# Order of the work around five RMS norms in a two-layer fp32 encoder: weight tiles ahead of the norm, modulation units behind it

## The chip, the cores and the metric

The kernel runs on one core of one Trainium2 chip. Its time is device microseconds from start to end of one execution, and runs are compared by their median.

## The reference

Two layers, 256 tokens, width 2048, everything in fp32. Each layer makes six vectors of 2048 values from a conditioning vector c, normalizes, modulates, mixes with two kinds of attention, and applies an MLP with a squared ReLU:

```python
c_act = jax.nn.silu(c)
for layer in range(DEPTH):                       # DEPTH = 2
    mod = c_act @ ada_w[layer] + ada_b[layer]    # 2048 -> 6 * 2048
    sh1, sc1, g1, sh2, sc2, g2 = split(mod, 6)
    h = rmsnorm(x, norm_mix[layer]) * (1 + sc1) + sh1
    proj = h @ w_in[layer]                       # 2048 -> 4608
    ...                                          # differential and windowed attention
    x = x + g1 * (concatenate([out_a, out_b]) @ w_out[layer])        # 2048 -> 2048
    h2 = rmsnorm(x, norm_mlp[layer]) * (1 + sc2) + sh2
    x = x + g2 * (square(relu(h2 @ w_up[layer])) @ w_down[layer])    # 2048 -> 8192 -> 2048
return rmsnorm(x, final_norm)
```

rmsnorm(x, g) is x / sqrt(mean(x^2) + 1e-6) * g over the width.

## The kernel before

x lies in SBUF with the features on partitions: 16 chunks of 128 features x 256 tokens, held as 8 pairs of chunks. A weight comes in raw tiles of 128 x 1024 fp32 (0.52 MB), issued on the queue of SyncE (SP) into a ring of six buffers. To keep fp32 accuracy each raw tile is split in two: ScalarE (ACT) casts it to `whi` (L367) and VectorE (DVE) makes the rest `wlo` = raw - whi (L368). Four such split tiles fit at a time. h is split alike into hi and lo. For each chunk and 128 columns, TensorE (PE) runs one matmul of `whi` against hi and lo side by side (512 columns, L408) and one of `wlo` against hi (256 columns, L410). A tile carries 512 output columns of two chunks, so 16 matmuls; a block of 512 columns over eight chunks is four tiles, 64 matmuls, and its four sums leave PSUM by ACT (L487) and DVE (L488).

The six modulation vectors of the two layers are computed beside this on DVE, in 384 units. One unit loads a 128 x 1024 tile of `ada_w` into the same ring of six buffers and reduces it against c_act with one long DVE instruction and a read of its accumulator (both L255). A layer's vectors are needed stage by stage, so units are mixed into the gemms: `pace(goal, tiles)` works out how many units go with each weight tile so that `goal` units are done when the stage ends, and `feed` issues them. The goals are the table GOALS, for the in-projection's two parts, w_out and the four parts of the MLP of each layer. Of a layer's 192 units the first 96 serve its mixer and the other 96 its MLP.

A stage ends in `residual` (L761: x = acc * gate + x on DVE), and the following norm squares x on ACT (L530), adds six of the eight squared pairs on DVE (L534), sums over features on PE with a matmul against a matrix of 1/2048 (L541), and takes (mean+eps)^-0.5 with Ln and Exp on ACT (L550, L551) and one Newton step of four DVE operations (L552 to L555). Then `modulated` makes h of pair i: x times r (L585, L587), hi and the unrounded v on ACT (L589, L593; v on DVE, L591, in layer 1), and lo = v - hi on DVE (L595, L599). There are five norms: at the start, before the MLP and before the mixer of layer 1, before that layer's MLP, and at the end. The names used below for the stages are: w_out0, w_up0 (the MLP of layer 0 up to its first goal of 160 units), mixer 1, w_out1, w_up1.

A list scheduler gives the order of the instructions on each engine from the order in which they were written and from priorities (the norm and h are written under a high priority); on the engine they run in that order, and a semaphore wait holds all that stands behind it.

Of the kernel before, what the change touches and what calls it, by code (L numbers as in the profile page):

```python
# [16 lines left out]
ALU = mybir.AluOpType  # L17
# [25 lines left out]
RAWB, WB = 6, 8  # L43


GOALS = [((72, 96, 120), (160, 204, 248, 304)), ((316, 326, 352), (384, 384, 384, 384))]
# [76 lines left out]
def encoder_trunk(  # L123
# [258 lines left out]

    def gemm(w, c0, width, rows, acts, kind, rate, banks=None, begin=True, end=True):
# [7 lines left out]
        tiles, index = w  # L391
# [57 lines left out]
        for u in range(0, n, per):  # L449
            raw = rawp.tile([P, RAW], F32, tag="raw", name=nm("raw"))  # L450
            nc.sync.dma_start(raw, tiles[index[(c0, rows[u])]])
            if acts[u][1]:
                hl = split(raw, RAW)
            for j in range(per):
                cs = slice(j * width, (j + 1) * width)
                if acts[u + j][1]:
                    held.append((u + j, hl[0][:, cs], hl[1][:, cs]))
                else:
                    held.append((u + j, raw[:, cs], None))
# [64 lines left out]
    ssq = [None, None]  # L524

    def square_sum(i):

        n = NCH // 2
        sq = tmp() if i else bslot(F32)[:, 0]
        nc.scalar.activation(sq, X[i], AF.Square)  # L530
        if i == 0:
            ssq[1] = sq
        elif i < SQ_ADDED:
            nc.vector.tensor_add(ssq[1], ssq[1], sq)  # L534
        if i < SQ_ADDED - 1:
            return
        if i == SQ_ADDED - 1:
            ssq[0] = misc_bank()
            sq = ssq[1]
        for j in range(2):  # L540
            nc.tensor.matmul(  # L541
                ssq[0][:, 0, :], lhsT=mean_d, rhs=sq[:, j, :],
                start=i == SQ_ADDED - 1 and j == 0, stop=i == n - 1 and j == 1, skip_group_check=True)

    def norm_x():

        ms = ssq[0][:, 0, :]
        t = bslot(F32)
        r, y, a = t[:, 0, 0, :], t[:, 0, 1, :], t[:, 1, 0, :]
        nc.scalar.activation(a, ms, AF.Ln, bias=eps)  # L550
        nc.scalar.activation(y, a, AF.Exp, scale=-0.5)  # L551
        nc.vector.tensor_mul(a, y, y)  # L552
        nc.vector.scalar_tensor_tensor(a, ms, EPS, a, op0=ALU.add, op1=ALU.mult)
        nc.vector.tensor_scalar(a, a, -0.5, 1.5, op0=ALU.mult, op1=ALU.add)
        nc.vector.tensor_mul(r, y, a)  # L555
        return r
# [16 lines left out]
    def modulated(l, sec, i, rstd, cols):  # L573
        whole = (l, sec, i) in WHOLE
        t = tmp()
        if whole:
            v = v0 = single()
        else:
            hl = bslot()
            v = tmp()  # L580
        hi, lo = (None, None) if whole else (hl[:, 0], hl[:, 1])
        for j in range(2):
            G, sh = cols[j]
            if i == 0:
# [3 lines left out]
            if not whole:  # L588
                nc.scalar.activation(hi[:, j, :], t[:, j, :], AF.Identity, scale=G, bias=sh)  # L589
            if (l, sec) in V_DVE:  # L590
                nc.vector.tensor_scalar(v[:, j, :], t[:, j, :], G, sh, op0=ALU.mult, op1=ALU.add)  # L591
            else:
                nc.scalar.activation(v[:, j, :], t[:, j, :], AF.Identity, scale=G, bias=sh)  # L593
            if i == 0 and not whole:
                nc.vector.tensor_tensor(lo[:, j, :], v[:, j, :], hi[:, j, :].bitcast(F32), op=ALU.subtract)  # L595
# [114 lines left out]
    def grouped_gemm(w, blocks, groups, get_act, goal, capped=None):  # L710
# [3 lines left out]
        for gi, gn in enumerate(groups):  # L714
# [7 lines left out]
            acts = [get_act(kk) for kk in rows]  # L722
            k0 += gn
            for bi, (c0, width, kind, finish) in enumerate(blocks):
# [7 lines left out]
                banks = gemm(w, c0, width, rows, acts, kind, r)  # L732
                if last:
# [32 lines left out]
    def mixer(l, groups, goals):  # L766
        with tc.high_priority():
            if l == 0:
                for i in range(NCH // 2):
                    square_sum(i)  # L770
            rstd = norm_x()
# [53 lines left out]
        grouped_gemm(w_in[l], blocks, groups, get_h, goals[0], (l, 0))  # L825
# [3 lines left out]
        rate = pace(goals[2], 32)  # L829
        for part in range(2):  # L830
# [3 lines left out]
            for c0 in range(0, D, w):  # L834
                banks = gemm(w_out[l], c0, w, rows, acts, kind, rate)
                residual(banks, l, 2, c0 // (2 * P), part == 1, kind)

    def mlp(l, groups, goals):
# [94 lines left out]
```

## Time and profile before

| | us |
|---|---|
| median of three runs | 2317.24 |
| the three runs | 2321.05, 2309.28, 2317.24 |
| the profiled execution, whole | 2310.85 |
| its span in the trace | 2309.1 |
| PE busy in the span | 2191.3 (95%) |
| DVE busy | 1808.1 (78%) |
| ACT busy | 1061.2 (46%) |

Busy is the time in which an engine ran at least one instruction. PE is close to full over the whole, but DVE is not evenly used: the units fill it in the first two thirds of the program, and after unit 384 it has less to do. A value of idle time ahead of an instruction says what ended that idle time.

### The profile page before, as it was taken

Reading aid. Unit: us, or ns where it says so; the run is one execution under the profiler, and the core shown is the slowest. Engines: PE = TensorE matmul, PEld = TensorE weight load, DVE = VectorE, ACT = ScalarE, POOL = GpSimd, SP = SyncE. Lnnn points to the kernel's source line nnn. Section 1 sums busy time; section 2 is a strip of 40 time slices with the busy share of each in tenths; the row PEclk is TensorE's granted clock in tenths of the full one; section 3 lists DMA queues with packets and bytes.
Section 4 is the critical chain, followed back from the end, with each engine's and each line's share of the span. In section 5 each row is a group of like instructions: output and inputs, shape, how many; then the busy total and the mean of one; then the engine's idle time right before and its main releaser. Section 6 shows DMA issues by size and latency. Waiting matters only on the chain.

```text
span 2309.1 us, 33300 instructions
## 1 busy us (share of the span) xinstructions
PE 2191.3 (95%) x12540; PEld 1894.8 (82%) x12540; DVE 1808.1 (78%) x2698; ACT 1061.2 (46%) x1521; POOL 0.2 (0%) x4
## 2 busy tenths in 40 slices
PE   5879999789999999999989999997999999999997
PEld 4768888678888888888878977886888888888886
DVE  6899899998888788988888578999886555565454
ACT  2436565355443334444336467534444334454442
POOL 0000000000000000000000000000000000000000
PEclk8989999999999999999999999999999999999999
DMA  8887675898678999999885754686886565555653
GB/s 324 327 311 275 217 255 201 293 329 301 204 274 316 316 317 328 314 338 348 312 302 192 246 182 157 211 290 236 297 282 233 185 195 186 192 191 187 195 184 110
DMA packets 162450, 585.96 MB, mean 254 GB/s; under 512 B 18289, under 2 KB 18801, under 8 KB 162289
## 3 DMA queue, kind: packets, MB, share of 16 engines
q1 hardware_dynamic: 162288, 583.83, 73.0%
q8 instruction: 99, 1.62, 0.3%
q14 instruction: 63, 0.51, 0.1%
HBM read 581.66 MB, written 2.10 MB: 253 GB/s over the span
## 4 chain that ended last, share of the span: by engine, by line
PE 83%; DVE 4%; ACT 2%; issue 1%; DMA 1%; ACTq 0%; DVEq 0%
PE acc L408 48%; PE acc L410 25%; PE acc L381 2%; PE acc L379 2%; PE acc L380 2%; PE misc L616 1%; DVE wlo L368 1%; PE lg L631 1%; DVE araw L255 1%; DVE x L761 1%; PE misc L608 1%; PE lg L680 1%; DMA raw<-in_w_up_dram 0%; ACT whi L367 0%; PE misc L562 0%
## 5 line engine op out<-in xcount | busy, mean ns | idle before, releaser
L408 PE MATMUL acc<-b,whi 128*128 128x512 f32 x4992 | 1742.5, 395 | 38.8 <-DVE b L595 29.4
L410 PE MATMUL acc<-b,wlo 128*128 128x256 f32 x4992 | 1377.1, 281 | 5.0 <-DVE wlo L368 4.8
L408 PEld LDWEIGHTS acc<-b,whi 128*128 128x128 f32 x4992 | 933.4, 188 | 249.2 <-issue 38.0
L367 ACT CAST whi<-raw 128x1024 fp32r<-128x1024 f32 x711 | 726.7, 1052 | 871.8 <-PE acc L408 540.0
L368 DVE TENSOR_TENSOR wlo<-raw,whi 128x1024 fp32r<-128x1024 f32 x711 | 851.9, 1222 | 321.5 <-ACT whi L367 319.4
L410 PEld LDWEIGHTS acc<-b,wlo 128*128 128x128 f32 x4992 | 943.5, 189 | 25.1 <-DVE wlo L368 11.9
L255 DVE CUSTOM_DVE_ANT_0 araw<-araw,c_act,vecs 128x1024 f32<-128x1024 f32 x192 | 249.1, 1303 | 43.5 <-DMA araw<-in_ada_dram 43.3
L255 DVE CUSTOM_DVE_ANT_0 araw<-araw,c_act,mod 128x1024 f32<-128x1024 f32 x192 | 249.1, 1303 | 35.5 <-DMA araw<-in_ada_dram 35.1
L761 DVE SCALAR_TENSOR_TENSOR x<-acc,mod,x 128x256 f32<-128x256 f32 x256 | 112.9, 480 | 24.1 <-PE acc L410 22.1
L379 PE MATMUL acc<-b,whi 128*128 128x256 f32 x320 | 92.1, 291 | 2.9 <-ACT whi L367 2.9
L380 PE MATMUL acc<-b,whi 128*128 128x256 f32 x320 | 91.8, 290 | 0.0
L381 PE MATMUL acc<-b,wlo 128*128 128x256 f32 x320 | 89.4, 293 | 2.5 <-DVE wlo L368 2.4
L487 ACT COPY tmp<-acc 128x256 f32<-128x256 f32 x120 | 44.5, 372 | 64.6 <-PE acc L410 64.3
L488 DVE TENSOR_TENSOR tmp<-tmp,acc 128x256 f32<-128x256 f32 x152 | 62.0, 418 | 14.0 <-ACT tmp L487 13.8
L498 ACT CAST b<-tmp 128x512 fp32r<-128x512 f32 x72 | 44.8, 623 | 49.8 <-DVE tmp L854 48.9
L379 PEld LDWEIGHTS acc<-b,whi 128*128 128x128 f32 x320 | 62.6, 196 | 4.9 <-ACT whi L367 3.3
L381 PEld LDWEIGHTS acc<-b,wlo 128*128 128x128 f32 x320 | 61.1, 197 | 5.3 <-DVE wlo L368 4.0
L380 PEld LDWEIGHTS acc<-b,whi 128*128 128x128 f32 x320 | 62.7, 196 | 1.1 <-issue 1.0
L380 PE MATMUL acc<-wlo,b 128*128 128x512 f32 (+1 forms) x152 | 56.6, 372 | 3.1 <-DVE wlo L368 3.0
L530 ACT ACTIVATE tmp<-x 128x512 f32<-128x512 f32 x35 | 21.7, 631 | 75.7 <-DVE x L761 68.3
L381 PE MATMUL acc<-whi,b 128*128 128x512 f32 (+1 forms) x152 | 55.9, 367 | 0.0
L499 DVE TENSOR_TENSOR b<-tmp,b 128x512 fp32r<-128x512 f32 x72 | 49.3, 688 | 7.1 <-ACT b L498 6.2
(156 smaller groups left out, 1258.6 us busy)
## 6 DMA issues: line engine op xcount, KB each, us to landing
araw<-in_ada_dram SPq DMA_DIRECT2D x384, 512.0 KB, 5.2
raw<-in_w_up_dram SPq DMA_DIRECT2D x256, 512.0 KB, 4.5
raw<-in_w_down_dram SPq DMA_DIRECT2D x256, 512.0 KB, 4.6
raw<-in_w_in_dram SPq DMA_DIRECT2D x144, 512.0 KB, 4.7
raw<-in_w_out_dram SPq DMA_DIRECT2D x64, 512.0 KB, 4.7
x<-in_x_dram SPq DMA_DIRECT2D x8, 256.0 KB, 5.0
out_dram<-tmp SPq DMA_DIRECT2D x8, 256.0 KB, 2.3
b<-in_diff_lambda_dram SPq DMA_DIRECT2D x1, 256.0 KB, 7.8
```

What stands on the lines that cost most here:

```text
L255: nc.vector.tensor_tensor_reduce(raw, raw, c_act[:, hf * RAW : (hf + 1) * RAW], scale=scale, scalar=m[:, ch : ch + 1] if hf else vecs[:, b ...
L367: nc.scalar.copy(hi, raw)
L368: nc.vector.tensor_tensor(lo, raw, hi.bitcast(F32), op=ALU.subtract)
L379: nc.tensor.matmul(o, lhsT=lhi, rhs=rhi, start=first, stop=False, skip_group_check=True)
L380: nc.tensor.matmul(o, lhsT=lhi, rhs=rlo, start=False, stop=False, skip_group_check=True)
L381: nc.tensor.matmul(o, lhsT=llo, rhs=rhi, start=False, stop=last, skip_group_check=True)
L408: nc.tensor.matmul(bank, lhsT=hi[:, fs], rhs=act[:, :, aj, :], start=first, stop=False, skip_group_check=True)
L410: nc.tensor.matmul(bank[:, 1, :], lhsT=lo[:, fs], rhs=act[:, 0, aj, :], start=False, stop=last, skip_group_check=True)
L488: nc.vector.tensor_add(tj, tj, b[:, 1, :])
L498: nc.scalar.copy(hl[:, 0], src)
L499: nc.vector.tensor_tensor(hl[:, 1], src, hl[:, 0].bitcast(F32), op=ALU.subtract)
L761: nc.vector.scalar_tensor_tensor(x[:, j, :], sums, g[j], x[:, j, :], op0=ALU.mult, op1=ALU.add)
```

## The change

- `load_ahead` issues and splits the first two raw tiles of w_up or of the next layer's w_in behind the last gemm block of w_out or w_down, ahead of that block's residual.
- No units go with that last block; the goals move, and the pace of the blocks before it is worked out over fewer tiles (28 of 32, 48 of 64).
- In the first block behind a norm (four tiles in w_up0), all that is written after h of pair 0 is queued behind the last ACT and the last DVE operation of the norm and of that h (`issue_after`).
- h of a pair is made when a tile needs it, two chunks ahead (`OnDemand`, LOOK), in place of a whole group at once.
- The Newton step takes three DVE operations, hi and v of pair 0 are made on DVE, the squares of the last pair are taken in two halves, and the first norm adds nothing on DVE: PE sums all 16 chunks.

```diff
-GOALS = [((72, 96, 120), (160, 204, 248, 304)), ((316, 326, 352), (384, 384, 384, 384))]
+AHEAD = 2
+LOOK = 2
+GOALS = [((72, 96, 116), (160, 208, 252, 296)), ((312, 324, 352), (384, 384, 384, 384))]
...
+    def load(w, c0, row, whole=False):
+        tiles, index = w
+        raw = rawp.tile([P, RAW], F32, tag="raw", name=nm("raw"))
+        nc.sync.dma_start(raw, tiles[index[(c0, row)]])
+        return (raw, None) if whole else split(raw, RAW)
+    class OnDemand:
+        def __init__(self, get, rows):
+            self.get, self.rows = get, rows
+        def __getitem__(self, i):
+            return self.get(self.rows[i])
+    def load_ahead(w, c0):
+        for row in range(0, 2 * AHEAD, 2):
+            ahead[(id(w), c0, row)] = load(w, c0, row)
...
         for u in range(0, n, per):
-            raw = rawp.tile([P, RAW], F32, tag="raw", name=nm("raw"))
-            nc.sync.dma_start(raw, tiles[index[(c0, rows[u])]])
-            if acts[u][1]:
-                hl = split(raw, RAW)
+            acts[min(u + LOOK, n - 1)]
+            key = (id(w), c0, rows[u])
+            hl = ahead.pop(key) if key in ahead else load(w, c0, rows[u], not acts[u][1])
...
+    @contextmanager
+    def behind(ops):
+        with ExitStack() as stack:
+            for op in ops:
+                stack.enter_context(tc.issue_after(op.ins))
+            yield
+    def square_sum(i, added=SQ_ADDED):
         n = NCH // 2
+        sq = tmp() if i or not added else bslot(F32)[:, 0]
+        if i == n - 1:
+            for j in range(2):
+                nc.scalar.activation(sq[:, j, :], X[i][:, j, :], AF.Square)
...
         nc.scalar.activation(a, ms, AF.Ln, bias=eps)
-        nc.scalar.activation(y, a, AF.Exp, scale=-0.5)
-        nc.vector.tensor_mul(a, y, y)
-        nc.vector.scalar_tensor_tensor(a, ms, EPS, a, op0=ALU.add, op1=ALU.mult)
-        nc.vector.tensor_scalar(a, a, -0.5, 1.5, op0=ALU.mult, op1=ALU.add)
-        nc.vector.tensor_mul(r, y, a)
+        last_op[1] = nc.scalar.activation(y, a, AF.Exp, scale=-0.5)
+        nc.vector.scalar_tensor_tensor(a, ms, EPS, y, op0=ALU.add, op1=ALU.mult)
+        nc.vector.scalar_tensor_tensor(a, a, -0.5, y, op0=ALU.mult, op1=ALU.mult)
+        last_op[0] = nc.vector.scalar_tensor_tensor(r, a, 1.5, y, op0=ALU.add, op1=ALU.mult)
         return r
...
+            if not whole and i == 0:
+                nc.vector.tensor_scalar(hi[:, j, :], t[:, j, :], G, sh, op0=ALU.mult, op1=ALU.add)
+            elif not whole:
                 nc.scalar.activation(hi[:, j, :], t[:, j, :], AF.Identity, scale=G, bias=sh)
-            if (l, sec) in V_DVE:
-                nc.vector.tensor_scalar(v[:, j, :], t[:, j, :], G, sh, op0=ALU.mult, op1=ALU.add)
+            if (l, sec) in V_DVE or i == 0:
+                last_op[0] = nc.vector.tensor_scalar(v[:, j, :], t[:, j, :], G, sh, op0=ALU.mult, op1=ALU.add)
...
+            acts = OnDemand(get_act, rows)
+            if gi == 0 and norm is not None:
+                acts[0]
+                front.enter_context(behind(last_op))
...
                 banks = gemm(w, c0, width, rows, acts, kind, r)
+                front.close()
...
-        rate = pace(goals[2], 32)
+        rate = pace(goals[2], 28)
...
-                banks = gemm(w_out[l], c0, w, rows, acts, kind, rate)
+                final = part == 1 and c0 + w == D
+                banks = gemm(w_out[l], c0, w, rows, acts, kind, 0.0 if final else rate)
+                if final:
+                    load_ahead(w_up[l], 0)
...
-            rate = pace(goal, n * 2)
+            rate = pace(goal, n * 2 - (n // 2 if final else 0))
...
+                quiet = final and nb == 3
+                banks = gemm(w_down[l], nb * 512, 512, rows, acts, "s", 0.0 if quiet else rate)
+                if quiet and l + 1 < DEPTH:
+                    load_ahead(w_in[l + 1], KA)
```

The instructions on DVE at the norm before w_up0 show the move. Before, from the end of the last residual (L761) to r (L555); b_4169 holds the norm's values, a line with araw is a unit, and the line after it its read:

```order
L255 ISA araw_4217,mod_3315<-araw_4217,c_act,vecs 128x1024
L255 ISA mod_3315 128x1
L552 TENSOR_TENSOR b_4169<-b_4169 128x256
L255 ISA araw_4220,mod_3325<-araw_4220,c_act,vecs 128x1024
L255 ISA mod_3325 128x1
L553 SCALAR_TENSOR_TENSOR b_4169<-misc_4049,b_4169 128x256
L255 ISA araw_4223,mod_3315<-araw_4223,c_act,mod_3315,vecs 128x1024
L255 ISA mod_3315 128x1
L554 TENSOR_SCALAR b_4169<-b_4169 128x256
L255 ISA araw_4226,mod_3325<-araw_4226,c_act,mod_3325 128x1024
L255 ISA mod_3325 128x1
L555 TENSOR_TENSOR b_4169<-b_4169 128x256
```

After, in the same place; L803 is the residual, L587 to L589 the Newton step, L619 to L636 h, L257 a unit:

```order
L803 SCALAR_TENSOR_TENSOR x_107<-acc_4054,mod_1503,x_107 128x256 x2
L587 SCALAR_TENSOR_TENSOR b_4172<-misc_4048,b_4172 128x256
L588 SCALAR_TENSOR_TENSOR b_4172<-b_4172 128x256
L589 SCALAR_TENSOR_TENSOR b_4172<-b_4172 128x256
L619 TENSOR_TENSOR tmp_4178<-x_93,b_4172 128x256 x2
L623 TENSOR_SCALAR b_4179<-tmp_4178,mod_3320,mod_3330 128x256
L627 TENSOR_SCALAR tmp_4180<-tmp_4178,mod_3320,mod_3330 128x256
L623 TENSOR_SCALAR b_4179<-tmp_4178,mod_3320,mod_3330 128x256
L631 TENSOR_TENSOR b_4179<-tmp_4180,b_4179 128x256
L627 TENSOR_SCALAR tmp_4180<-tmp_4178,mod_3320,mod_3330 128x256
L631 TENSOR_TENSOR b_4179<-tmp_4180,b_4179 128x256
L621 TENSOR_TENSOR tmp_4193<-x_95,b_4172 128x512
```

The units that stood between the norm's operations have gone behind h of pair 0. They come back a little later on the same engine; this is the end of the first block's list in the changed kernel, between the x * r of pair 3 (tmp_4282) and the splits (L370) of the third and the fourth tile:

```order
L257 ISA araw_4276,mod_3320<-araw_4276,c_act,mod_3320,vecs 128x1024
L257 ISA mod_3320 128x1
L257 ISA araw_4279,mod_3330<-araw_4279,c_act,mod_3330 128x1024
L257 ISA mod_3330 128x1
L621 TENSOR_TENSOR tmp_4282<-x_99,b_4172 128x512
L370 TENSOR_TENSOR wlo_4294<-raw_4291,whi_4293 128x1024
L257 ISA araw_4297,mod_3320<-araw_4297,c_act,vecs 128x1024
L257 ISA mod_3320 128x1
L636 TENSOR_TENSOR b_4283<-tmp_4284,b_4283 128x512
L257 ISA araw_4300,mod_3330<-araw_4300,c_act,vecs 128x1024
L257 ISA mod_3330 128x1
L370 TENSOR_TENSOR wlo_4306<-raw_4303,whi_4305 128x1024
```

From the norm's last operation to the lo of pair 3 (L636 of tmp_4284) 14 units stand in the changed order. Before, 9 stand from the end of the residual to the lo of pair 3, 6 of them ahead of r.

On the SP queue the changed kernel issues this around the same norm:

```order
L389 DMA raw_4099<-in_w_out_dram 128x1024
L389 DMA raw_4105<-in_w_out_dram 128x1024
L389 DMA raw_4143<-in_w_up_dram 128x1024
L389 DMA raw_4149<-in_w_up_dram 128x1024
L250 DMA araw_4202<-in_ada_dram 128x1024
L250 DMA araw_4205<-in_ada_dram 128x1024
L250 DMA araw_4208<-in_ada_dram 128x1024
L250 DMA araw_4211<-in_ada_dram 128x1024
L250 DMA araw_4214<-in_ada_dram 128x1024
L250 DMA araw_4258<-in_ada_dram 128x1024
L250 DMA araw_4261<-in_ada_dram 128x1024
L250 DMA araw_4264<-in_ada_dram 128x1024
```

The last two tiles of w_out, two of w_up, and then units alone, where the order before had units between the tiles of w_out's last block.

## Rows read from the trace of the kernel before

**Rows 1.** The page's first part: busy us, share, instructions of each engine.
```profile
PE 2191.3 (95%) x12540; PEld 1894.8 (82%) x12540; DVE 1808.1 (78%) x2698; ACT 1061.2 (46%) x1521; POOL 0.2 (0%) x4
```

**Rows 2.** Waits: who waited for whom, us in total, times, longest.
```profile
PE acc L408 <- DVE b L595: 29.4, 3, 10.9
...
DVE araw L255 <- DMA araw<-in_ada_dram: 78.3, 65, 3.4
```

**Rows 3.** Stage ends: instructions of PE in time (start, length us; [idle <-releaser]).
```profile
450.08 0.28 PE L410 MATMUL acc<-b,wlo 128*128 128x256 f32 x1
...
465.26 0.77 PE L408 MATMUL acc<-b,whi 128*128 128x512 f32 x1 [10.93 <-DVE b L595]
...
1194.65 0.28 PE L410 MATMUL acc<-b,wlo 128*128 128x256 f32 x1
...
1206.83 0.76 PE L408 MATMUL acc<-b,whi 128*128 128x512 f32 x1 [7.87 <-DVE b L595]
...
1566.73 0.28 PE L410 MATMUL acc<-b,wlo 128*128 128x256 f32 x1
...
1581.21 0.76 PE L408 MATMUL acc<-b,whi 128*128 128x512 f32 x1 [10.58 <-DVE b L595]
```

**Rows 4.** DVE in time, at the norm before w_up0 and in the block behind it.
```profile
452.39 1.34 DVE L255 CUSTOM_DVE_ANT_0 araw<-araw,c_act,mod 128x1024 f32<-128x1024 f32 x1
...
453.65 1.29 DVE L255 CUSTOM_DVE_ANT_0 araw<-araw,c_act,mod 128x1024 f32<-128x1024 f32 x1
...
460.67 0.43 DVE L555 TENSOR_TENSOR b<-b 128x256 f32<-128x256 f32 x1
...
471.96 2.38 DVE L368 TENSOR_TENSOR wlo<-raw,whi 128x1024 fp32r<-128x1024 f32 x2
...
479.00 0.42 DVE L488 TENSOR_TENSOR b<-b,acc 128x256 f32<-128x256 f32 x1 [0.74 <-ACT b L487]
```

**Rows 5.** The final norm in time, where no units are left.
```profile
2294.77 0.28 PE L410 MATMUL acc<-b,wlo 128*128 128x256 f32 x1
2295.09 1.00 DVE L761 SCALAR_TENSOR_TENSOR x<-acc,mod,x 128x256 f32<-128x256 f32 x2 [1.20 <-PE acc L410]
2296.13 0.63 ACT L530 ACTIVATE tmp<-x 128x512 f32<-128x512 f32 x1 [2.54 <-DVE x L761]
2296.81 1.13 PE L541 MATMUL misc<-tmp,mean_d 128*128 128x256 f32 x4 [1.76 <-ACT tmp L530]
...
2300.18 0.42 DVE L555 TENSOR_TENSOR b<-b 128x256 f32<-128x256 f32 x1
```

**Rows 6.** Groups of instructions: count, busy us and mean ns, idle before.
```profile
L591 DVE TENSOR_SCALAR tmp<-tmp,mod,mod 128x256 f32<-128x256 f32 x32 | 11.8, 417 | 0.0
L599 DVE TENSOR_TENSOR b<-tmp,b 128x512 fp32r<-128x512 f32 x28 | 19.5, 696 | 3.4 <-ACT b L589 1.9 <-ACT tmp L593 1.3
```

**Rows 7.** Stretches: us, busy us of PE, PEld, DVE, ACT, POOL; clock, DMA share, GB/s.
```profile
20.00:60.00 40.00, 28.72 (x84) 19.89 (x84) 30.15 (x51) 8.62 (x16) 0.00 (x0) 0.82 0.89 332
400.00:450.00 50.00, 45.93 (x256) 38.87 (x256) 48.70 (x77) 16.66 (x20) 0.00 (x0) 1.00 0.82 283
480.00:560.00 80.00, 73.50 (x400) 60.41 (x399) 75.22 (x110) 37.01 (x55) 0.00 (x0) 1.00 0.95 354
540.00:560.00 20.00, 18.52 (x106) 15.66 (x105) 17.23 (x25) 10.70 (x16) 0.00 (x0) 1.00 0.97 372
560.00:600.00 40.00, 40.00 (x232) 35.00 (x231) 33.12 (x52) 23.34 (x34) 0.00 (x0) 1.00 0.59 193
1477.00:1567.00 90.00, 88.34 (x491) 74.86 (x490) 86.78 (x147) 35.95 (x49) 0.00 (x0) 1.00 0.78 268
```

**Rows 8.** The start in time: PE's first norm matmuls and gemm, and a unit.
```profile
20.88 2.07 PE L541 MATMUL misc<-b,mean_d 128*128 128x256 f32 x4 [11.42 <-DVE b L534]
...
29.32 2.08 PE L377 MATMUL acc<-b,raw 128*128 128x256 f32 x4 [3.81 <-ACT b L593]
...
29.48 1.34 DVE L255 CUSTOM_DVE_ANT_0 araw<-araw,c_act,vecs 128x1024 f32<-128x1024 f32 x1
```

More of the change, by code (lines that the diff above doesn't have):

```diff
@@ L2 @@
 from collections import deque
-from contextlib import ExitStack, nullcontext
+from contextlib import ExitStack, contextmanager, nullcontext
 import numpy as np
@@ L381, in mm3 @@
         nc.tensor.matmul(o, lhsT=llo, rhs=rhi, start=False, stop=last, skip_group_check=True)
+    def load(w, c0, row, whole=False):
[8 more added lines that the diff above has]
+            return self.get(self.rows[i])
+    ahead = {}
+    def load_ahead(w, c0):
+        for row in range(0, 2 * AHEAD, 2):
+            ahead[(id(w), c0, row)] = load(w, c0, row)
     def gemm(w, c0, width, rows, acts, kind, rate, banks=None, begin=True, end=True):
-        tiles, index = w
         if banks is None:
@@ L542, in square_sum @@
                 ssq[0][:, 0, :], lhsT=mean_d, rhs=sq[:, j, :],
-                start=i == SQ_ADDED - 1 and j == 0, stop=i == n - 1 and j == 1, skip_group_check=True)
+                start=i == first and j == 0, stop=i == n - 1 and j == 1, skip_group_check=True)
     def norm_x():
@@ L708, in chunks_of, with grouped_gemm @@
         return [(hl, split_, j) for hl in pairs for j in range(2)]
-    def grouped_gemm(w, blocks, groups, get_act, goal, capped=None):
+    def grouped_gemm(w, blocks, groups, get_act, goal, capped=None, norm=None):
         accs = [None] * len(blocks)
@@ L721, in grouped_gemm @@
             rows = list(range(k0, k0 + gn))
-            acts = [get_act(kk) for kk in rows]
+            front = ExitStack()
+            acts = OnDemand(get_act, rows)
+            if gi == 0 and norm is not None:
+                acts[0]
+                front.enter_context(behind(last_op))
             k0 += gn
@@ L824, in mixer @@
             blocks.insert(KV_AT[l], late[0])
-        grouped_gemm(w_in[l], blocks, groups, get_h, goals[0], (l, 0))
+        grouped_gemm(w_in[l], blocks, groups, get_h, goals[0], (l, 0), True)
         if KV_AT[l] >= 0:
@@ L858, in up @@
             grouped_gemm(w_up[l], [(c0 + j, 512, "s", fin_up) for j in range(0, ncols, 512)],
-                         groups, get_h, goal, (l, 3))
+                         groups, get_h, goal, (l, 3), True if c0 == 0 else None)
         def down(k0, n, goal, final):
-            rate = pace(goal, n * 2)
+            rate = pace(goal, n * 2 - (n // 2 if final else 0))
             acts = chunks_of(u[k0 // 2 : (k0 + n) // 2])
@@ L865, in down @@
             for nb in range(4):
-                banks = gemm(w_down[l], nb * 512, 512, rows, acts, "s", rate)
+                quiet = final and nb == 3
+                banks = gemm(w_down[l], nb * 512, 512, rows, acts, "s", 0.0 if quiet else rate)
+                if quiet and l + 1 < DEPTH:
+                    load_ahead(w_in[l + 1], KA)
                 residual(banks, l, 5, nb * 2, final)
```

24 lines of the change are left out of this document (11 added, 13 removed).

## Prediction

> **What bounds the kernel now.** I read the busy shares first: PE is busy 95% of the span [rows 1], so the 118 us in which it isn't are all that a reordering can win. The waits come next. Three waits of PE for lo of pair 0 cost 29.4 us, and DVE waits 78.3 us for the loads of units [rows 2]. The first says that stage ends hurt; the second that units are held by their DMA too. Then the instructions in time at the stage ends. Take T as the end of a stage's last gemm matmul. The first gemm matmul of the next stage starts 14.9 us later before w_up0 (450.36 to 465.26), 11.9 us at mixer 1 and 14.2 us at w_up1 [rows 3]. Before w_up0, DVE runs one unit after the other there, 1.26 us from start to start, and r is done at 461.10, T+10.7 [rows 4]. At the final norm, where no unit is left, r is done at 2300.60, T+5.55 [rows 5]. So about 5 us of the 10.7 are units in the norm's way, and the remaining 4 us of the gap are h.
>
> Last, I ask of each stretch who has slack, because a unit that is moved still has to run. In 480 to 560 us, behind that norm, DVE is busy 75.2 of 80 us and PE misses 6.5 us; as soon as the units' goal is met, in 560 to 600, PE misses nothing and DVE has 7 us to spare. In 400 to 450 (w_out0) DVE is busy 48.7 of 50, PE misses 4.1; in 1477 to 1567 (w_out1) DVE 86.8 of 90, PE misses 1.7 [rows 7]. Around the norms DVE is the bound, not the norm's chain; what the chain gives up reappears if DVE has the same list to run.
>
> **The new gap.** The residual's last part takes 1.0 us, and from the start of the square to the end of r the final norm takes 4.5 us [rows 5]. With a half square (0.63 becomes about 0.45), two of PE's four sums behind it (1.13 becomes 0.55) and three Newton operations for four (0.45 less), that is 3.3; behind 1.0 of residual r comes at T+4.4, and I take T+4.5. h of pair 0 then runs on DVE alone: two x*r, two hi, one v and one lo of about 0.4 us [rows 4, 6], steps overlapping to about 2.2: first matmul at T+6.7. That is 8.2, 5.2 and 7.5 us less than the three gaps, 20.9 in all, if nothing else stood in the way. The rest of the working is what the pushed work takes back; each term is PE time gained (+) or lost (-).
>
> **Start: +2 (-2 to +6).** PE's norm matmuls no longer wait 11.4 us for DVE adds, and the gemm could start some 6 us before 29.32. But a unit runs on DVE at 29.48 [rows 8], the ones behind it are the same, and DMA loads them at the same rate. Only a part stays.
>
> **w_out0: +2 (0 to +4.1).** 19 units in seven blocks, and 0 in the last, replace 23 in eight. Four units less are 5 us of DVE in a stage where PE missed 4.1 us in 50 [rows 7]; half of it.
>
> **w_up0 up to unit 160: -9 (-15 to +8).** The 14 units between r and the lo of pair 3 now stand inside the first block. DVE's list from its second lo, at T+7.1, to the lo of pair 3: 14 units at 1.26 (17.6), six operations of 512 columns at 0.6 (3.6), one split 1.14: T+29.4. One unit and the fourth tile's split follow (T+32), and that tile's 16 matmuls take 2.8 (64 matmuls, a block, 11.2). So the block ends at T+35. Before, it ends at about T+29: its third eviction is at 479.00, T+28.6 [rows 4]. Net -6: the gap shrinks by 8.2 and the block grows by 14. The blocks behind it: before, about 5 units in each, 4 splits at 1.19, 4 evictions at 0.42: 12.7 us of DVE for 11.2 of PE. Now unit 160 must be reached after 24 tiles in place of 26, about 5.5 units a block: 13.4. Over 5.3 blocks the 0.63 costs 3.3. Together -9.3. As a check, 80 us of this stretch lost PE 6.5 us at the old density. The upper end is the whole 8.2 of the gap; the lower is DMA below.
>
> Loading is the second limit in this block. The stretch 540 to 560 moved 372 GB/s, the 80 us around it 354 [rows 7]. A block of 9.5 tiles of 0.524 MB is 4.98 MB: 13.4 us at the first rate, 14.1 at the second. At the first it is equal to DVE's 13.4, and I take no extra. The Trainium skill ("DMA: Bandwidth & Descriptors", Where 436 GB/s comes from) puts the memory limit of one core at about 358 GB/s. By that page a block would take an estimated 13.9 us, and the sum would be 2.7 us worse; the row at 372 GB/s lies above that figure, so the measurement decides here, if only over 20 us.
>
> **Mixer 1: +2 (-1 to +5.2), w_up1: +2 (-1 to +7.5).** Here few units stand behind the norm (one or two a block), but all eight pairs' h is DVE work: in layer 1 v is on DVE too, at 417 ns, and lo at 696 [rows 6]. After T+4.5 for w_up1: pair 0 2.6, seven pairs at about 1.9 (13.2), six splits 6.8, four units 5.0: T+32.1, the last tile 2.8: T+34.9. The same list before, with its first matmul at T+14.2 and 8 tiles (22.4) plus its waits, comes to T+38. That is 3 of the 7.5; 1 goes in the next block, whose splits stand later. Mixer 1 likewise.
>
> **w_out1: -4.5 (-9 to 0).** Its 25 units go in seven blocks, against 23 in eight. DVE ran 86.8 us in eight blocks, so 75.9 for seven, plus 25 - 20.1 units at 1.26: 82.1, and at before's density (0.964) 85.2 us for 78.4 of PE. The last block adds 11.2 at PE's speed: 96.4 against 90 [rows 7]. The four tiles that may be split ahead give back some 2 to 4; I take -4.5 of the 6.4.
>
> **Final norm: +1 (+0.5 to +1.5).** One DVE step and half a square less in rows 5's chain, with nothing to push.
>
> **Sum.** 2 + 2 - 9.3 + 2 + 2 - 4.5 + 1 = -4.8: the profiled execution of 2310.85 (its span 2309.1 and 1.75 around it) would become about 2315.7. That execution lies 6.4 below the median of the runs, 2317.24, and inside their spread; by the median the change gives 2322. This is 0.2%, less than the 0.5% (11.6 us) that I take as what a measurement here tells from no change.
>
> **Rivals.**
> (a) *The gaps close and the pushed units find room.* 8.2 + 5.2 + 7.5 + 2 + 1 = 23.7: 2293.5. For it: rows 2's 29.4 us is a true wait on the path, and DVE waits 78.3 us for unit loads over the program, so its busy time isn't all it can do; the loads of the units would go on while the norm runs. Against it: the ring has six buffers, so behind two w_up tiles only some six unit loads can be done during the norm, and the 75.2 of 80 in [rows 7] comes right after.
> (b) *Loading becomes the bound behind the norm* (the slower side). In the block after the norm before w_up0, the units come as one run behind two w_up tiles on SP, and the third w_up tile is queued behind 14 of them. With no DVE during the norm to free buffers, loads stop for up to 6 us where before they ran on. If then 5.3 blocks of 4.98 MB go at the 332 GB/s of 20 to 60 us, another stretch full of units [rows 7], a block takes 15.0, 1.6 us more than DVE: 8.5, with half of the 6 us (3) and 3 at w_out1 14.5, so 2336. It decides from the point at which loading falls below 372 GB/s. Against it: that rate over 20 us, and 354 over 80.
> (c) *Only the order changes.* DVE loses ten operations (five Newton steps, five adds) and gains ten (hi and v of pair 0); if DVE is the bound throughout the units' stretches, the block sums come out equal and only start and end count, 3 us: 2314.
> The half clock after a gap goes with (a): the first matmul after the gap at w_up0 takes 0.77 us [rows 3]. A gap short enough to keep the clock would win about 2 us more each, but only where the block is not bound by DVE.
>
> **How the numbers follow.** Forecast 0.45, (a) 0.25, (b) 0.18, (c) 0.12. The predicted time is 2321, between the median's 2322 and 2320 by the mean of all four executions. Its own range is 2311 to 2331. The 8-in-10 range reaches to (a)'s centre and (b)'s: 2292 to 2337. Faster than 2305.6: most of (a) (0.22), and 0.04 from the forecast's tail, 0.26. Slower than 2328.8: most of (b) (0.15) and 0.09 from the forecast, where w_up0 or w_out1 come out at their lower ends: 0.24. Within: 0.50.
>
> **What would show it.** First gemm matmul at T+6.7 at the three norms: the new gap is right. First block before w_up0 ending at T+35 with PE waiting for lo of pair 3 or `wlo`: the push is right; at T+24 or less, (a). PE's idle time in the six blocks after it: above 12 us for the forecast, near 6 for (a), above 18 with loads as the releaser for (b). w_out1's seven blocks at over 82 us: its term is right. r in the final norm at T+4.6. The prediction is wrong if DVE, after the norm, catches up the units without holding a split: then DVE's idle time before was larger than the busy shares show.

## The result: about 1% slower, just outside the range

The changed kernel ran at 2340.1 us (median of 4, 2332.66 to 2344.28), the kernel before in the same comparison at 2313.3: a ratio of 1.0112, interval 1.0067 to 1.0157. Seven more runs of the changed kernel gave 2336.5 and 1.0100 (1.0071 to 1.0128). The forecast was 2321 with a range of 2292 to 2337; 2340.1 lies outside it, on the slow side.

The changed kernel's page, first part, and its waits (us in total, times, longest) answer to [rows 1, 2]:

```profile
PE 2219.3 (95%) x12560; PEld 1902.8 (81%) x12560; DVE 1805.1 (77%) x2698; ACT 1054.3 (45%) x1516; POOL 0.2 (0%) x4
```
```profile
DVE araw L257 <- DMA araw<-in_ada_dram: 83.5, 53, 4.8
...
PE acc L434 <- DVE wlo L370: 16.9, 24, 3.8
PE acc L432 <- ACT whi L369: 14.2, 6, 10.3
PE acc L432 <- DVE b L631: 13.7, 3, 4.6
...
PE acc L432 <- DVE tmp L508: 4.5, 7, 1.2
```

The wait that the change aims at went from 29.4 us to 13.7. In its place PE waits for the two halves of a weight tile (L369, L370) and for evictions (L508). PE's idle time in all is nearly the same (2309.1 - 2191.3 = 117.8 us before, 119.6 after); it is *busy* 28 us longer, with 20 matmuls more.

PE's rows at the three stage ends in layer order [rows 3]:

```profile
446.23 0.28 PE L434 MATMUL acc<-b,wlo 128*128 128x256 f32 x1
...
453.33 0.77 PE L432 MATMUL acc<-b,whi 128*128 128x512 f32 x1 [4.58 <-DVE b L631]
...
472.02 2.08 PE L432 MATMUL acc<-b,whi 128*128 128x512 f32 x4 [10.33 <-ACT whi L369]
...
1212.95 0.28 PE L434 MATMUL acc<-b,wlo 128*128 128x256 f32 x1
...
1220.05 0.77 PE L432 MATMUL acc<-b,whi 128*128 128x512 f32 x1 [4.58 <-DVE b L631]
...
1594.17 0.28 PE L434 MATMUL acc<-b,wlo 128*128 128x256 f32 x1
...
1601.28 0.76 PE L432 MATMUL acc<-b,whi 128*128 128x512 f32 x1 [4.58 <-DVE b L631]
```

With T = 446.51 the first gemm matmul before w_up0 comes at T+6.8 (forecast T+6.7, before T+14.9); at mixer 1 and w_up1 it comes at T+6.8 too (before T+11.9 and T+14.2). Then, before w_up0, the third tile is missing, and PE stands 10.3 us until 472.02. DVE in that block [rows 4]:

```profile
450.67 0.43 DVE L589 SCALAR_TENSOR_TENSOR b<-b 128x256 f32<-128x256 f32 x1
...
475.35 0.69 DVE L636 TENSOR_TENSOR b<-tmp,b 128x512 fp32r<-128x512 f32 x1
...
479.56 1.22 DVE L370 TENSOR_TENSOR wlo<-raw,whi 128x1024 fp32r<-128x1024 f32 x1
480.69 1.41 DVE L508 TENSOR_TENSOR b<-b,acc 128x256 f32<-128x256 f32 x4
```

r is done at T+4.6, the lo of pair 3 at T+29.5, and the evictions behind the block start at T+34.2 (forecast T+4.5, T+29.4, T+35). DVE is never idle in between. The third raw tile was held as well: its load is issued at 466.30, behind nine units on SP whose buffers come free only as DVE reads them. From 446 to 456 DMA moved next to nothing (2 GB/s; before, from 445 to 460, 321 GB/s).

Two stretches that answer to [rows 7], behind the norm and in w_out1, and one in w_up1 where the kernel before keeps PE full:

```profile
490.00:575.00 85.00, 76.64 (x410) 61.69 (x409) 74.87 (x109) 41.82 (x67) 0.00 (x0) 1.00 0.93 339
...
1504.00:1594.00 90.00, 85.73 (x465) 71.20 (x464) 85.75 (x137) 32.68 (x37) 0.00 (x0) 1.00 0.84 291
...
1700.00:1790.00 90.00, 86.97 (x490) 74.65 (x489) 66.59 (x88) 40.74 (x55) 0.00 (x0) 1.00 0.78 258
```

In the last row DVE has 23 us to spare and PE still misses 3. The first row reaches 25 us past unit 160; 481 to 560, to set beside 480 to 560 in [rows 7], moved 363 GB/s at a DMA share of 0.98, with DVE busy 74.2 of 79 us.

The final norm [rows 5]: r at 2330.41, T+4.57 for T+5.55.

```profile
2325.56 0.28 PE L434 MATMUL acc<-b,wlo 128*128 128x256 f32 x1
...
2329.99 0.42 DVE L589 SCALAR_TENSOR_TENSOR b<-b 128x256 f32<-128x256 f32 x1
```

**Where the time went.** Both programs run the same 4992 matmuls of `whi` (L408 before, L432 after), so the start of the n-th in one trace less its start in another gives the delay at each point of the program. The first profiled execution of before is the reference; negative is faster. The columns are the experiments of the next section in their order: "changed 1" is the trace above, "changed 2" and "before 2" the second traces of the two kernels, "best 1" the old plan with the queueing in layer 1 alone, "best 2" that with eight units more in the in-projection.

| us, by matmul n | changed 1 | changed 2 | before 2 | no queueing | old units | exact | exact, old goals | best 1 | best 2 |
|---|---|---|---|---|---|---|---|---|---|
| up to 256: end of w_out0 | -3.8 | -0.5 | -4.0 | -5.0 | -0.1 | -4.3 | -0.1 | +0.4 | +5.0 |
| 256-512: w_up0, unit 160 | +9.9 | +9.2 | -1.2 | +5.5 | +3.0 | +6.8 | +1.8 | -0.8 | -9.4 |
| 512-1792: MLP 0 | +8.4 | +1.3 | +1.2 | 0.0 | 0.0 | 0.0 | +8.4 | +2.3 | +5.1 |
| 1792-2304: last w_down0 | +3.7 | +3.1 | +0.2 | +1.3 | +0.2 | +5.2 | +14.9 | +1.5 | +1.4 |
| 2304-2432: mixer 1, norm | -3.3 | -3.5 | +0.1 | -0.5 | -3.4 | -4.7 | -5.3 | -3.3 | -3.7 |
| 2432-2688: rest of mixer 1 | +5.8 | +1.1 | +0.2 | +2.6 | +0.2 | -0.2 | 0.0 | +0.5 | +0.1 |
| 2688-2944: w_out1 | +6.6 | +7.1 | +0.5 | +6.7 | +0.6 | +6.7 | +4.1 | +0.5 | -0.9 |
| 2944-3072: w_up1, norm | -3.1 | -3.1 | +1.4 | -1.8 | -2.5 | -3.7 | -3.6 | -2.4 | -2.4 |
| 3072-3456: w_up1, to unit 384 | +6.1 | +5.6 | 0.0 | +10.1 | 0.0 | 0.0 | 0.0 | 0.0 | 0.0 |
| 3456 to the end | -0.5 | -0.5 | 0.0 | +9.0 | -0.5 | -0.5 | -0.2 | -0.5 | -0.5 |
| sum | +29.8 | +19.9 | -1.6 | +27.8 | -2.5 | +5.4 | +20.0 | -1.6 | -5.4 |

A slower pace of PE, which comes and goes from one execution to the next (see the first experiment), is in these numbers too: it alone can make 8.4 us in the row 512-1792 and 3.4 in the row 1792-2304.

The gaps at the norms got shorter, and the loss lies in the blocks behind and between them.

### The profile page after: what moved, and what is told of

Same layout as the page of the kernel before. It is cut to its first block, busy times and chain, and to the rows that moved or that the text cites. A ratio compares the mean times of both kernels' runs of the same rounds, so it can differ in the third digit from the quotient of the medians.

```text
span 2338.9 us, 33333 instructions
## 1 busy us (share of the span) xinstructions
PE 2219.3 (95%) x12560; PEld 1902.8 (81%) x12560; DVE 1805.1 (77%) x2698; ACT 1054.3 (45%) x1516; POOL 0.2 (0%) x4
## 4 chain that ended last, share of the span: by engine, by line
PE 72%; DVE 10%; DMA 4%; issue 3%; ACT 2%; DVEq 0%; ACTq 0%
PE acc L432 42%; PE acc L434 21%; DMA araw<-in_ada_dram 3%; DVE wlo L370 3%; DVE araw L257 3%; PE misc L653 1%; PE lg L668 1%; PE acc L383 1%; PE acc L382 1%; PE acc L381 1%; DMA raw<-in_w_up_dram 1%; DVE x L803 1%; PE misc L645 1%; PE lg L717 1%; PE misc L576 1%
## 5 line engine op out<-in xcount | busy, mean ns | idle before, releaser
L432 PE MATMUL acc<-b,whi 128*128 128x512 f32 x4992 | 1756.8, 398 | 36.6 <-ACT whi L369 14.2
L432 PEld LDWEIGHTS acc<-b,whi 128*128 128x128 f32 x4992 | 934.9, 189 | 257.2 <-issue 22.1
L369 ACT CAST whi<-raw 128x1024 fp32r<-128x1024 f32 x711 | 724.6, 1049 | 885.9 <-PE acc L432 556.8
L370 DVE TENSOR_TENSOR wlo<-raw,whi 128x1024 fp32r<-128x1024 f32 x711 | 849.4, 1220 | 343.7 <-ACT whi L369 341.1
L257 DVE CUSTOM_DVE_ANT_0 araw<-araw,c_act,mod 128x1024 f32<-128x1024 f32 x192 | 248.4, 1299 | 45.3 <-DMA araw<-in_ada_dram 44.9
L257 DVE CUSTOM_DVE_ANT_0 araw<-araw,c_act,vecs 128x1024 f32<-128x1024 f32 x192 | 248.4, 1299 | 39.2 <-DMA araw<-in_ada_dram 38.7
L803 DVE SCALAR_TENSOR_TENSOR x<-acc,mod,x 128x256 f32<-128x256 f32 x256 | 112.6, 478 | 26.2 <-PE acc L434 24.5
L508 DVE TENSOR_TENSOR tmp<-tmp,acc 128x256 f32<-128x256 f32 x152 | 61.2, 416 | 10.1 <-ACT tmp L507 9.8
L383 PE MATMUL acc<-whi,b 128*128 128x512 f32 (+1 forms) x152 | 55.8, 367 | 0.0
L381 PE MATMUL acc<-whi,b 128*128 128x512 f32 (+1 forms) x152 | 53.3, 372 | 1.4 <-ACT whi L369 1.1
```

The costliest lines, as they stand in the source:

```text
L257: nc.vector.tensor_tensor_reduce(raw, raw, c_act[:, hf * RAW : (hf + 1) * RAW], scale=scale, scalar=m[:, ch : ch + 1] if hf else vecs[:, b ...
L369: nc.scalar.copy(hi, raw)
L370: nc.vector.tensor_tensor(lo, raw, hi.bitcast(F32), op=ALU.subtract)
L381: nc.tensor.matmul(o, lhsT=lhi, rhs=rhi, start=first, stop=False, skip_group_check=True)
L383: nc.tensor.matmul(o, lhsT=llo, rhs=rhi, start=False, stop=last, skip_group_check=True)
L432: nc.tensor.matmul(bank, lhsT=hi[:, fs], rhs=act[:, :, aj, :], start=first, stop=False, skip_group_check=True)
```

## The experiments

Ratios are to the kernel before, run beside each group of experiments (medians 2313.3, 2312.5 and, for the last three, 2315.9 us). Two theories at the start: *push* (what stands behind the norm holds the first block) and *density* (the new plan puts too many units into too few tiles); a third, *phase*, came out of the first four runs.

**The changed kernel and the kernel before once more** (no edit).

> The changed kernel once more. In its first trace PE ran one matmul pair per 353 ns instead of 347 from 575 to 1090 us without being idle, which cost 0.42 us in each block of 64 matmuls, about 10 us. Theory 'execution' (which of the two paces PE falls into is a matter of the single execution): the pace in that stretch comes out at 347 in some executions, and the time of such a one is some 10 us lower; the median may fall anywhere from 2328 to 2344. Theory 'kernel' (the order of the changed kernel fixes the pace): 353 again in the same stretch, median 2335 to 2345. Both expect the rest to repeat: the first block before w_up0's goal ends 7 us later against the end of w_out0 than before, the next three blocks lose 3 more, w_out1 loses 6 to 7.

> The kernel before, once more, for a second trace. Theory 'execution': 353 ns per matmul pair can show in the MLP of layer 0 or 1 here too, and the time then lies near 2321, otherwise near 2307. Theory 'kernel': 347 in 575 to 1090 us again, and 353 again only in 1325 to 1525 us, as in the first trace.

Measured: 2336.5 (1.0100, 1.0071 to 1.0128) and 2313.6 (0.9997, 0.9967 to 1.0027). The stretch 800 to 1000 us, first of the changed kernel's first trace, then of its second:

```profile
800.00:1000.00 200.00, 200.00 (x1133) 173.47 (x1132) 173.15 (x233) 87.20 (x109) 0.00 (x0) 1.00 0.90 317
```
```profile
800.00:1000.00 200.00, 200.00 (x1155) 176.36 (x1154) 174.93 (x236) 88.54 (x112) 0.00 (x0) 1.00 0.92 323
```

PE is busy throughout at the full granted clock in both, and runs 22 matmuls fewer in the first. So 7 us of the first trace's loss (8.4 in the row 512-1792 for 1.3) belong to that execution, not to the change, as *execution* expected; the second trace of the kernel before, with 1.2 there, doesn't decide it. The other stages repeat within 1 us, but for the attention (5.8 and 1.1) and the start.

**Without the queueing behind the norm.**

```diff
             if gi == 0 and norm is not None:
                 acts[0]
-                front.enter_context(behind(last_op))
```

> The changed kernel without the queueing behind the norm: eight or nine units stand between the residual and r before w_up0 again, all else as changed. Theory 'push' (units queued behind h of pair 0 hold the third tile's split): the first gemm matmul comes later, at T+13 or so instead of T+6.7, but the first block ends 2 to 5 us earlier than with the queueing, because DVE and the loads no longer stand idle during the norm; in all 3 to 6 us faster than the changed kernel. Rival 'density' (what costs is that unit 160 falls due two tiles sooner and the last block of w_out takes none): the end of the first block doesn't move by more than 1.5 us, and the time is that of the changed kernel. Rival 'chain' (the queueing is what wins): 3 to 8 us slower.

Measured: 2340.7, 1.0098 (1.0062 to 1.0135). *Push* held before unit 160 alone: 5.5 us lost in place of 9.2 to 9.9. The run lost most of the gain of mixer 1 (0.5 for 3.3) and part of w_up1's (1.8 for 3.1), and 10.1 in 3072-3456 for 6, of which 2.4 are the slower pace; that pace then lasts to the end (+9.0). The time stayed, so the queueing isn't what makes the change slow.

**Units planned as before, the rest changed.**

```diff
-GOALS = [((72, 96, 116), (160, 208, 252, 296)), ((312, 324, 352), (384, 384, 384, 384))]
+GOALS = [((72, 96, 120), (160, 204, 248, 304)), ((316, 326, 352), (384, 384, 384, 384))]
...
-        rate = pace(goals[2], 28)
+        rate = pace(goals[2], 32)
...
-                banks = gemm(w_out[l], c0, w, rows, acts, kind, 0.0 if final else rate)
+                banks = gemm(w_out[l], c0, w, rows, acts, kind, rate)
...
-            rate = pace(goal, n * 2 - (n // 2 if final else 0))
+            rate = pace(goal, n * 2)
...
-                banks = gemm(w_down[l], nb * 512, 512, rows, acts, "s", 0.0 if quiet else rate)
+                banks = gemm(w_down[l], nb * 512, 512, rows, acts, "s", rate)
```

> The changed kernel with the units planned as before: the old goals, units in a stage's last block too, paced over all tiles; tiles split ahead, queueing, Newton step and h as changed. Theory 'density': about 5 units fewer stand behind the norm before w_up0, so its first block ends some 6 us earlier and the next three lose 3 less; w_out1 gets its 6 us back; in all 10 to 16 us faster than the changed kernel, near 2325. Rival 'push': the units that are left behind the norm still hold the third split; 3 to 6 us faster. Rival 'chain': the units of the last block stand in the way of the residual again, no change within 3 us.

Measured: 2313.0, 0.9997 (0.9979 to 1.0016). The whole loss goes with the plan of the units, more than *density* expected. That w_up1 recovered its 6 us was not explained by it: there the unit counts are the same to one (353 done at its start in the changed kernel, 352 here).

**Exact credits.** `feed` adds the share of a unit to a credit with each tile and issues one when it reaches 1. With 20 units over 28 tiles the sum of the shares ends just under 1: in the changed kernel a unit is left over after w_out of layer 0 (115 done at the start of w_up0, for 116), and the credit of almost 1 is carried along. In w_up1 it makes each unit come one tile earlier, behind the first tile of a pair. After w_out of layer 1 no unit is left over; there one too many is done (353 for 352). The old plan's shares, over 32 and 64 tiles, add up exactly, so the run before has no rounding either.

```diff
-        while credit[0] >= 1.0:
+        while credit[0] >= 1.0 - 1e-6:
```

> The changed kernel, with the units' credit compared to 1 less a millionth. In the changed kernel the sum of 28 shares ends at 0.99999, so a unit is left over at the end of w_out and is issued one tile late: the units then stand behind the first tile of each pair in w_up1 in place of the second, and 45 in place of 44 go into the 32 tiles before unit 160. Theory 'phase' (where in a pair of tiles the unit stands decides whether its load is in time): the 5.6 us that the changed kernel loses in blocks 3 to 12 of w_up1 against the kernel before go to 0 to 1; 5 to 8 us faster than the changed kernel in all, near 2329. Rival 'density' (how many units, not where): under 1.5 us anywhere, and the time is 2335 to 2340.

Measured: 2320.1, 1.0039 (1.0015 to 1.0063). The loss in 3072-3456 is gone and a good part of the whole. More went than *phase* said: before unit 160, where 44 units stand in place of 45, 2.4 to 3.1 us less. The rest of mixer 1 no longer loses either: -0.2, where the traces with the rounded credits lost 1.1 to 5.8.

**Exact credits and the old goals, but no units in a last block.** The edit is the last one and GOALS as in the run before it.

> The changed kernel with the old goals (120 and 160, 304, 326 and 352, 384) and exact credits, but still without units in a stage's last block. Theory 'quiet' (the units taken out of the last block crowd the seven blocks ahead of it): w_out1 still loses 5 to 7 us and w_out0 gains nothing; before unit 160 no more than e_units loses, 3 us; 2320 to 2327 in all. Rival 'goals' (the moved goals cost): w_out1 within 2 us of the kernel before, the whole near 2313.

Measured: 2332.0, 1.0068 (1.0043 to 1.0094), 8.4 us of its trace by the slower pace. *Quiet* was half right: w_out1 loses 4.1, a little under what was expected, and the time is over its 2320 to 2327. The largest loss was not expected: 14.9 in the last w_down0, where 56 units in 48 tiles replace 56 in 64. w_up0 comes out as with the old plan.

**The old plan, with the queueing in layer 1 alone.**

```diff
-                         groups, get_h, goal, (l, 3), True if c0 == 0 else None)
+                         groups, get_h, goal, (l, 3), True if c0 == 0 and l else None)
```

> The changed kernel with the units planned as before, and the queueing behind the norm kept in layer 1 alone, where one or two units are near a norm; before the MLP of layer 0 units may stand in the norm again. Theory 'push': the 3 us that remain lost before unit 160 with queueing go to 0 to 1.5, while mixer 1 and w_up1 keep their gains of 3.5 and 2 to 3: 2 to 4 us under the run with queueing everywhere, 2307 to 2311, or 3 to 6 under the kernel before. Rival 'chain': the gap before w_up0 grows from 8 back to 13 to 15 us and its block ends as much later: 2315 to 2318.

Measured: 2308.5, 0.9964 (0.9939 to 0.9989): 0.4% faster than the kernel before and faster than the changed one, as *push* expected. PE before w_up0: the last matmul of w_out0, the first of w_up0 and the last of its first block:

```profile
450.50 0.28 PE L434 MATMUL acc<-b,wlo 128*128 128x256 f32 x1
...
467.04 0.76 PE L432 MATMUL acc<-b,whi 128*128 128x512 f32 x1 [13.01 <-DVE b L631]
...
480.69 0.28 PE L434 MATMUL acc<-b,wlo 128*128 128x256 f32 x1
```

The same three with the queueing there, in the run with the old plan before:

```profile
449.95 0.28 PE L434 MATMUL acc<-b,wlo 128*128 128x256 f32 x1
...
458.06 0.77 PE L432 MATMUL acc<-b,whi 128*128 128x512 f32 x1 [4.58 <-DVE b L631]
...
480.17 0.28 PE L434 MATMUL acc<-b,wlo 128*128 128x256 f32 x1
```

From the end of w_out0 the gap is 16.3 us without and 7.8 with the queueing, and the first block ends after 30.2 us in both. DVE's list is the block.

**Eight units more in the in-projection**, on top of that: goals 76, 104, 124 for 72, 96, 120.

> As the last one, with eight units more in the in-projection of layer 0 (goals 76, 104, 124 for 72, 96, 120), so that 36 in place of 40 go into the 32 tiles before unit 160. Theory 'density': these tiles gain 4 units of 1.26 us, some 4 to 5 us, and the attention, where DVE has 9 of 50 us to spare from 250 to 300, takes the eight for nothing to 2 us: 2304 to 2309. Rival 'bound elsewhere' (DVE or loading is as tight in the in-projection as behind the norm): what is won before unit 160 is lost there, 2308 to 2314.

Measured: 2308.0, 0.9975 (0.9955 to 0.9995). Before unit 160 it gains 9.4 us on the kernel before, more than expected; 5.0 us are lost ahead of it, but the traces of the other kernels scatter from -6.2 to +0.4 there, so that the size of this price is open. In time it isn't told apart from the last one.

**Only the place of the units in w_up1**, in the kernel before.

```diff
     def mlp(l, groups, goals):
+        if l == 1:
+            credit[0] = 0.5
```

> The kernel before with one number set: the units' credit is 0.5 at the start of the MLP of layer 1, so that the 32 units there stand behind the first tile of each pair in place of the second; nothing is split ahead, queued or added. Theory 'phase': w_up1 from its second block to its sixteenth or so, where the kernel before never lets PE wait, loses 4 to 7 us, with DVE waiting for a unit's load once in each pair of tiles (5 to 7 us in 22) instead of for ACT's cast; the whole near 2318. Rival 'backlog' (the changed kernel's loss there came from what the norm and w_out1 left behind, not from the place): under 1 us, time as before.

Measured: 2328.2, 1.0055 (1.0025 to 1.0085); 7.3 us lost in 3072-3456, 6.1 of it around PE's waits and the rest by the slower pace (*phase* expected 4 to 7). Ahead of that, where nothing was edited, the trace lost 3.7 and 2.6 us in MLP 0 to the slower pace, and from 3456 on 10.1 more. The whole is 10 us over the 2318 expected. DVE in w_up1 there, then in the kernel before:

```profile
1711.70 2.36 DVE L368 TENSOR_TENSOR wlo<-raw,whi 128x1024 fp32r<-128x1024 f32 x2
1716.49 1.28 DVE L255 CUSTOM_DVE_ANT_0 araw<-araw,c_act,vecs 128x1024 f32<-128x1024 f32 x1 [2.43 <-DMA araw<-in_ada_dram]
...
1724.86 0.41 DVE L488 TENSOR_TENSOR tmp<-tmp,acc 128x256 f32<-128x256 f32 x1
1727.53 1.28 DVE L255 CUSTOM_DVE_ANT_0 araw<-araw,c_act,mod 128x1024 f32<-128x1024 f32 x1 [2.25 <-DMA araw<-in_ada_dram]
...
1728.74 0.75 DVE L488 TENSOR_TENSOR tmp<-tmp,acc 128x256 f32<-128x256 f32 x2
```
```profile
1691.24 0.41 DVE L488 TENSOR_TENSOR tmp<-tmp,acc 128x256 f32<-128x256 f32 x1
1691.57 1.28 DVE L255 CUSTOM_DVE_ANT_0 araw<-araw,c_act,vecs 128x1024 f32<-128x1024 f32 x1
...
1692.77 0.90 DVE L488 TENSOR_TENSOR tmp<-tmp,acc 128x256 f32<-128x256 f32 x2
```

In both a unit stands between the first and the second eviction. In the kernel before it is there already, and the second eviction comes 1.5 us after the first. With the unit's place moved by one tile its load isn't there, DVE stands 2.25 us in front of it, and the second eviction comes 3.9 us after the first; PE wants that bank for the next block. PE's wait for it is 1.04 us here, until 1729.20; the same wait one block earlier:

```profile
1705.29 0.50 PE L408 MATMUL acc<-b,whi 128*128 128x512 f32 x1 [0.52 <-DVE tmp L488]
```

From 1640 to 1765 DVE waits 28.7 us for units' loads here; in the kernel before 1.8, and 22.6 for ACT's cast. It is not a matter of bandwidth: PE's share of the stretch, in this kernel, and DMA at 271 GB/s:

```profile
1700.00:1750.00 50.00, 48.44 (x276) 41.69 (x274) 37.71 (x52) 22.30 (x31) 0.00 (x0) 1.00 0.79 271
```

**The place put back**, in the changed kernel.

```diff
     def mlp(l, groups, goals):
+        if l == 1:
+            credit[0], issued[0] = 0.0, 352
```

> The changed kernel with the units of the MLP of layer 1 put back behind the second tile of each pair, 31 of them, and all else as changed, the rounding in the other stages too. Theory 'phase': the 5.6 us lost in w_up1 go to 0 to 1, all earlier losses stay: 2329 to 2334. Rival 'backlog': they stay, 2335 to 2340.

Measured: 2323.0, 1.0029 (0.9998 to 1.0060). 3072-3456 loses 0.0; the other stages stay as in the changed kernel (+9.4 before unit 160, +7.7 in w_out1). PE is full again in the stretch that answers to the last row:

```profile
1710.00:1760.00 50.00, 50.00 (x290) 43.72 (x289) 39.33 (x52) 23.14 (x31) 0.00 (x0) 1.00 0.84 284
```

The median fell by 14 us and more (2336.5 and 2340.1 to 2323.0), further than these 5.6; in its trace the start is 5.7 earlier than in the changed kernel's second, which the edit doesn't touch. One thing that may be in it: of the thirteen traces four have waits of PE in 3072-3456, and two of these four (without the queueing, and the place alone) keep the slower pace from there to the end, 9.0 and 10.1 us; none of the nine without waits does. Two of four is too few to show it.

**Units in all eight blocks of w_out1**, exact credits, the rest changed.

```diff
-        rate = pace(goals[2], 28)
+        rate = pace(goals[2], 32 if l else 28)
...
-                banks = gemm(w_out[l], c0, w, rows, acts, kind, 0.0 if final else rate)
+                banks = gemm(w_out[l], c0, w, rows, acts, kind, 0.0 if final and not l else rate)
```

> The changed kernel with exact credits, and in w_out of layer 1 alone the units spread over all eight blocks again (28 of them, the goals not moved back). Theory 'crowding' (28 units in seven blocks is over what DVE can do, in eight it is not quite): w_out1 loses 2 to 4 us against the kernel before in place of 6.7, and the norm behind it has 3 to 4 units around it, which costs its gain of 3.7 up to 1 us; 2317 to 2319 in all. Rival 'goals' (28 units where 26 were is what costs): w_out1 still loses 5 or more, and the time stays at 2320.

Measured: 2322.8, 1.0018 (0.9985 to 1.0051), its trace with 8.4 us of slower pace. w_out1 loses 1.2 us in place of 6.7, less than *crowding* expected, with the same 28 units; the norm behind it gains 2.5 in place of 3.7. The ratio isn't told apart from the 1.0039 of the run with exact credits, so this is shown by the stage alone.

## Why the prediction was wrong

The sum had the right sign and a quarter to a sixth of the size of the two traces. By its own terms, gain positive, against the two traces of the changed kernel:

| term | forecast | trace 1 | trace 2 |
|---|---|---|---|
| start and w_out0 | +4 | +3.8 | +0.5 |
| w_up0 to unit 160 | -9.3 | -9.9 | -9.2 |
| mixer 1, norm and two blocks | +2 | +3.3 | +3.5 |
| w_out1 | -4.5 | -6.6 | -7.1 |
| w_up1, norm and two blocks | +2 | +3.1 | +3.1 |
| final norm, with w_down1 | +1 | +0.5 | +0.5 |
| *not in the sum:* MLP 0 from 512 | 0 | -12.1 | -4.4 |
| *not in the sum:* rest of mixer 1 | 0 | -5.8 | -1.1 |
| *not in the sum:* w_up1 to unit 384 | 0 | -6.1 | -5.6 |

- **Right:** r at T+4.5, the first matmul at T+6.7, the first block at T+35 (T+4.6, T+6.8, evictions from T+34.2), and that DVE's list decides there. The price before unit 160, forecast 9.3, was 9.2 to 9.9: 5.4 in the first block (forecast 6) and 3.8 to 4.5 behind it (3.3). The two runs on the old plan, with the queueing and without it, end the block alike, as reasoned. One sign failed: PE's idle time in the six blocks behind was 9.0 us, not above 12 (8.4 in the second trace).
- **The step that failed** is the opening of the sum, "each term is PE time gained (+) or lost (-)", over stages at the norms alone. The goals and the empty last blocks also change every unit stage behind them. The stretches that were given nothing lost 11.1 us in the second trace, of the 15.1 by which it misses the sum; the terms that were worked out miss by 3.9, most of it w_out1 and the start. The largest of the 11.1 is w_up1 up to unit 384 (5.6). The last w_down0 lost 3.1, part of which can be the slower pace; that the plan costs there shows in the run with exact credits (5.2, at the faster pace) and in the one with 56 units in 48 tiles (14.9). The rest are MLP 0 before it (1.3, the pace) and the rest of mixer 1 (1.1).
- **The cause in w_up1** is the place of the units: the changed order has each one tile earlier in its pair of tiles, and its load isn't there in time. That could have been seen in the changed order; the 78.3 us of waits for units' loads in the trace of before [rows 2] were no sign of it, since only 5.9 of them lie in w_up1 (1581 to 1765). "1 goes in the next block, whose splits stand later" counted units and not their place. The edit in the kernel before (7.3 lost, 6.1 of it waits) and its reverse (0.0) settle it.
- **w_out1** was mis-sized: 6.6 to 7.1 for 4.5. Without the 2 to 4 us of return that the lead of split tiles was given, the working said 6.4; that the lead returns nothing fits this, but no run leaves the lead out. With 26 units in eight blocks the loss is 0.6, with 28 in eight 1.2, with 26 in seven 4.1, with 28 in seven 6.7: the seven blocks are most of it, the two units the rest. The sign set for the term, seven blocks at over 82 us, can't tell: they took 96.0 us, and 91.4 in the kernel before, whose whole w_out1 takes 104 and not the 90 of the window used.
- **Rival (b)** came near the time by luck, though parts of it held. Loads did stop at the norm (446 to 456), and the third tile's load was late, because its buffer waited for DVE, which had no idle time. In the blocks behind, 481 to 560 moved 363 GB/s at a DMA share of 0.98 with DVE busy 74.2 of 79 us, against 354, 0.95 and 75.2 of 80 before: whether DVE or the loads held these blocks is open. But they lost 3.8 to 4.5 us, not 8.5, and much of the measured loss lies in stretches that (b) doesn't touch. Rival (a) fell: the gaps shrank by 8.1, 5.1 and 7.4 us, and before w_up0 DVE's list took it all back; at mixer 1 and w_up1, with few units, 3.1 to 3.5 us were kept. The shorter gap won no clock either: from 453.3 to 458.6 the granted clock was 0.50 (1.2 GHz), and the first matmul took 0.77 us as before. (c) was nearest for the change without its plan of units: 2313.0.
- **The start** gained nothing that lasts: the first gemm matmul comes about 4 us earlier, but the traces at the end of w_out0 scatter from -6.2 to +0.4 with the change and from -4.0 to +0.1 without. w_out0 by itself, from its first matmul to its last, takes 115.2 to 117.5 us with the moved goals and 117.4 to 118.7 with before's order.

Open: how the rest of mixer 1 loses its 1.1 to 5.8 us. It goes with the rounded credits (the four traces that have them lost 1.1, 2.6, 3.2 and 5.8, all others -1.0 to +0.5), but no wait was traced.

## What to carry to other kernels

Sum a change of a schedule over every stretch whose rate or order it touches, not only over those it aims at; here what lay between cost about as much as the stage that was worked out best. Where filler work has loads of its own, its place among the main tiles counts as well as its number: look in the trace for the wait on its load, and in the new order for which side of it the tile stands. A gap of PE at a stage end is worth closing only where the engine that feeds the next block has slack; with a full list it is paid back within the block.

## What the hardware showed

PE ran the same pair of matmuls (512 and 256 columns) in 347 ns or in 353 ns on average from start to start, without idle time and at a granted clock of 1.00 in both. It keeps a pace for hundreds of us: the stretch from matmul 512 to 1792 of MLP 0 took 443.9 us in five of thirteen traces and 452.3 in three, of three different kernels, and lay between in the others. A short wait of PE often stands where the pace changes, but not always, and the same kernel showed both. This makes 8 us and more of spread between runs of one kernel, and a profile in which PE is "busy" longer is not yet a slower program. What sets the pace was not found.
